# Both halves of the S5 channel groups through one scan of double width

## Chip, cores and metric

The kernel runs on one core of one Trainium2 chip. The metric is the device time of one execution in microseconds (us), of which the median of several runs is taken. All times inside an execution are counted from the start of its profiled span.

## What is computed

The reference is one inference step of a hybrid decoder trunk of two layers, for a prompt of 512 positions and 8 sample sequences of one position (520 columns). Layer 0 begins with the mixer that this change is about:

```python
# even l: parallel head groups from ONE combined input projection D -> [u 512 | q 512 | f 512 | i 512 | g 512]
#   A = S5 diagonal SSM (32 groups x 16 channels, each group drives a 64-dim complex state, associative scan, Re(C h) + D u, GLU)
#   B = HGRN2 (4 heads), concat(A, B) (1024) -> ONE output projection
bu_r = einsum('gpc,nlgc->nlgp', bbr, uf)      # and bu_i
h_t  = a * h_(t-1) + bu_t                     # complex, per group and state
y    = einsum('gcp,nlgp->nlgc', c_re, xr) - einsum('gcp,nlgp->nlgc', c_im, xi) + d * u
z    = gelu(y);  out = z * sigmoid(z @ w_glu + b_glu)
```

After it come cross-attention into 256 memory tokens and a ConvFFN, then layer 1 with a Conformer module, cross-attention and ConvFFN. The kernel also returns the last states.

## The kernel before

The columns stay on the free axis and channels on the 128 partitions, so x is a tile of 8 x 520 columns. Every projection multiplies in three parts: a weight block that comes by DMA (`wraw`) is rounded by ScalarE (`whi`) and the rest is kept (`wlo`, on VectorE, or on POOL for the blocks named in `GW`); per block that gives 48 matmuls of 256 or 264 columns on TensorE (L203).

S5 runs in `mixer0` (L409). The recurrence is cut into 64 blocks of 8 positions. `in_u` (L443) writes the projected channels u; `s5_u` (L635) sends them through DRAM into a tile U that has channel and position in block on the partitions. `s5_powers` (L494) makes the powers of the decay. The 32 channel groups are worked in two halves of 16, each by these steps:

- `s5_ops` (L560): X, six products of 128x1024 on VectorE; their transposes pM on TensorE (L578), copied to M by ScalarE; pK (L586), the block's kernel taps from X and cbd, copied to KT; eight shifted copies of KT by DMA (kts, L596), scaled into the Toeplitz operand TP by eight ScalarE copies (L599); and E (`s5_E`, L607), six instructions on POOL.
- `s5_scan` (L648): pS, M times U (L661); ScalarE copies them to W and Ws; then on VectorE the scan inside a block (seven W steps of five instructions), the scan over blocks (seven Bs steps of five instructions), the products m of powers and block states, half of them on POOL, and Hs. Four DMAs (L722) turn Hs into Hst. VectorE also makes the sample state (o_s_s).
- `s5_emit` (L725): pY, for each of 16 groups E times Hst (L737) plus TP times U (L738); ScalarE copies Y, which goes through DRAM (yd) into `s5_out` (L747).

`fill` (L811) puts ph blocks of the HGRN2 projection between these steps, 4 before the first half, 6 after its scan and 5 after the second, the rest after the last pY: the constant `FILL`. After all that `s5_glu` (L764) multiplies by w_glu (pg) and the HGRN2 part begins.

The order in which each engine takes its instructions is not the order of the lines. The framework sorts them when the kernel is built, by a time line of its own; each engine then takes its queue in order, and waits where an operand is late. SP issues the DMAs, and a DMA there waits for the one that was issued eight places before.

Of the kernel before, what the change touches and what calls it, by code (L numbers as in the profile page):

```python
# [9 lines left out]
F32 = mybir.dt.float32  # L10
F32R = mybir.dt.float32r
# [7 lines left out]
P = 128  # L19
# [3 lines left out]
NB = 8  # L23
# [14 lines left out]
ELATE = 0  # L38
# [8 lines left out]
FILL = (4, 6, 5)  # L47
# [54 lines left out]
def trunk(ctx, tc, I, O, dbg=None):  # L102
# [306 lines left out]
    def mixer0(nxt):  # L409
# [28 lines left out]
        with ExitStack() as es:  # L438
# [55 lines left out]
            def s5_powers():  # L494
# [48 lines left out]
                b1 = s5.tile([P, 16, 16], F32, tag="sop", name="b1", bufs=6)  # L543
                b2 = s5.tile([P, 16, 16], F32, tag="sop", name="b2", bufs=6)
# [14 lines left out]

            def s5_ops(hf):  # L560
                js = slice(hf * 8, hf * 8 + 8)
                X = [s5.tile([P, 8, 16, 8], F32, tag="sop", name=f"X{i}", bufs=6) for i in range(2)]
# [4 lines left out]
                t = s5.tile([P, 8, 16, 8], F32, tag="sop", name="tX", bufs=6)  # L567
# [6 lines left out]
                M = [s5.tile([P, 8, P], F32, tag="sop", name=f"M{i}", bufs=6) for i in range(2)]  # L574
# [5 lines left out]
                cbd = s5.tile([P, 2, 8, 32], F32, tag="cbd", name="cbd", bufs=1)  # L580
# [9 lines left out]
                TP = s5.tile([P, 16, 16, 8], F32, tag="TP", name="TP", bufs=1)  # L590
                for tq in range(2):
                    raw = s5.tile([P, 4, 256], F32, tag="sop", name="kts", bufs=6)
                    G.memset(raw[96:P], 0.0)
                    for t4 in range(4):
                        sh = 7 - (tq * 4 + t4)
                        nc.sync.dma_start(raw[0:P - sh, t4], KT[sh:P])  # L596
                    for t4 in range(4):
                        t8 = tq * 4 + t4
                        act(TP[:, :, :, t8], raw[:, t4].rearrange("p (g c) -> p g c", c=16), AF.Copy,  # L599
                            scale=tmask[:, t8:t8 + 1])  # L600
                ops[hf] = M, TP
                if not ELATE:
                    s5_E(hf)

            Es = {}

            def s5_E(hf):  # L607
                js = slice(hf * 8, hf * 8 + 8)
                full = [P, 8, 16, 8]
                E = []  # L610
                for g2 in range(2):
                    po = [POs[:, i, g2, js, :][:, :, None, :].to_broadcast(full) for i in range(2)]
                    cc = [sp[:, o:o + 512].rearrange("p (g j c) -> p g j c", g=2, c=16)[:, g2, js, :, None]
                          .to_broadcast(full) for o in (S_CA, S_CB)]
                    e = s5.tile([P, 8, 16, 8], F32, tag="sop", name=f"E{g2}", bufs=6)
                    t = s5.tile([P, 8, 16, 8], F32, tag="sop", name="tE", bufs=6)
# [4 lines left out]
                Es[hf] = E  # L621
# [13 lines left out]
            def s5_u(hf):  # L635
                U = s5.tile([P, 16, U5], F32, tag="U", name="U", bufs=2)
                G.memset(U[:, :, 0:NB], 0.0)
                G.memset(U[:, :, NB + NK5:U5], 0.0)
                Us[hf] = U
# [4 lines left out]
                nc.sync.dma_start(U[:, :, NB:NB + NK5], by_pos(ud, hf))  # L644
                nc.sync.dma_start(U[7:P:8, :, 0:NB], by_chan(uds, hf))
                nc.sync.dma_start(U[0:P:8, :, NB + NK5:U5], by_chan(uds, hf))

            def s5_scan(hf):  # L648
                M, TP = ops[hf]
                U = Us[hf]  # L650
                j0 = hf * 8
                js = slice(j0, j0 + 8)
                W = s5.tile([P, 2, 8, 64], F32, tag="WH", name="W", bufs=1)
                Ws = s5.tile([P, 2, 8, NB], F32, tag="Ws", name="Ws", bufs=1)
                for i in range(2):
# [3 lines left out]
                    for j in range(8):  # L659
                        for g2 in range(2):  # L660
                            T.matmul(pv[g2 * 64:g2 * 64 + 64, j // 4, j % 4, :],  # L661
                                     M[i][:, j, g2 * 64:g2 * 64 + 64], U[:, 2 * j + g2, 0:H5],
                                     start=True, stop=True)
                    for b in range(2):
                        act(Ws[:, i, b * 4:b * 4 + 4, :], pv[:, b, :, 0:NB], AF.Copy)
# [5 lines left out]
                a8r = PA[:, 0, 1, js]  # L671
                a8i = PA[:, 1, 1, js]
                nai = s5.tile([P, 8], F32, tag="nai", name="nai", bufs=2)
                ts(V, nai, a8i, -1.0, None, MUL)
                t1 = s5.tile([P, 2, 8, 8], F32, tag="t1", name="t1", bufs=2)
                t2 = s5.tile([P, 2, 8, 8], F32, tag="t2", name="t2", bufs=2)
# [7 lines left out]
                B = s5.tile([P, 2, 9, 8], F32, tag="Bs", name="Bs", bufs=1)  # L684
                G.memset(B[:, :, 0, :], 0.0)
                V.tensor_copy(B[:, :, 1, :], Wv[:, :, 7, :, 0])
                b8r, b8i = PA[:, 0, 8, js], PA[:, 1, 8, js]
                nbi = s5.tile([P, 8], F32, tag="nbi", name="nbi", bufs=2)
                ts(V, nbi, b8i, -1.0, None, MUL)
                for b in range(1, 8):  # L690
                    hp = B[:, :, b, :]
                    tt(V, t1[:, :, :, 0], hp, b8r[:, None, :].to_broadcast([P, 2, 8]), MUL)
# [4 lines left out]
                nc.sync.dma_start(O["p_s5"][:, :, js], B[:, :, 8, :])  # L697
                Hs = s5.tile([P, 2, 8, H5], F32, tag="HY", name="Hs", bufs=1)
                Hv = Hs[:, :, :, :NK5].rearrange("p i j (b q) -> p i q j b", q=8)
                f7 = [P, 7, 8, 8]  # L700
                Bv = [B[:, i, 0:8, :].rearrange("p b j -> p j b")[:, None].to_broadcast(f7) for i in range(2)]
                Pv = [PA[:, i, 1:8, js][:, :, :, None].to_broadcast(f7) for i in range(2)]
                m = [s5.tile([P, 2, 7, 8, 8], F32, tag="sop", name=f"m{i}", bufs=6) for i in range(2)]
                for k in range(2):
                    tt(G, m[1][:, k], Pv[k], Bv[1 - k], MUL)
                    tt(V, m[0][:, k], Pv[k], Bv[k], MUL)
                for i in range(2):
                    G.tensor_copy(Hv[:, i, 0], B[:, i, 0:8, :].rearrange("p b j -> p j b"))
                    tt(V, m[i][:, 0], m[i][:, 0], m[i][:, 1], ADD if i else SUB)
                    tt(V, Hv[:, i, 1:8], m[i][:, 0], Wv[:, i, 0:7], ADD)  # L710
                h0 = sp[:, S_H0:S_H0 + 256].rearrange("p (i j b) -> p i j b", i=2, b=NB)[:, :, js, :]
                V.tensor_copy(Hs[:, :, :, NK5:], h0)
                a1 = [PW[:, i, 1, js][:, :, None].to_broadcast(f3) for i in range(2)]
                sh = s5.tile([P, 2, 8, NB], F32, tag="shs", name="shs", bufs=1)
                cmul(V, sh[:, 0], sh[:, 1], h0[:, 0], h0[:, 1], a1[0], a1[1], t1[:, 0], t1[:, 1])
                tt(V, sh, sh, Ws, ADD)
                nc.sync.dma_start(O["s_s5"][:, :, js, :], sh)

                Hst = s5.tile([P, 2, 8, H5], F32, tag="WH", name="Hst", bufs=1)
                for i in range(2):  # L720
                    for g2 in range(2):
                        nc.sync.dma_start(Hst[i * 64:i * 64 + 64, g2], Hs[g2 * 64:g2 * 64 + 64, i])  # L722
                return Hst

            def s5_emit(hf, Hst):  # L725
                (M, TP), E = ops[hf], Es[hf]
                U = Us[hf]
                Y = s5.tile([P, 16, H5], F32, tag="HY", name="Y", bufs=1)
                for gq in range(2):
# [3 lines left out]
                    for g8 in range(8):  # L733
# [4 lines left out]
                        T.matmul(o, TP[:, g].rearrange("p c t -> p (c t)"), U[:, g, NB:U5],  # L738
# [8 lines left out]
            def s5_out(c):  # L747
                y = s5.tile([P, NT], F32, tag="sop", name="y5", bufs=6)
# [9 lines left out]
            def s5_split(z):  # L758
                t = s5.tile([P, 2, NT], F32R, tag="sop", name="zsp", bufs=6)
# [73 lines left out]
            fill(FILL[2])  # L833
            if ELATE:
                s5_E(1)
            s5_emit(1, H)
# [8 lines left out]
        with ExitStack() as es:  # L845
# [172 lines left out]

            for h in range(HH):
                prepare(h)  # L1020
# [673 lines left out]
```

## Time and profile before

| what | value |
|---|---|
| three runs | 1762.98, 1769.52, 1767.95 us; median 1767.95 us |
| profiled execution | 1769.77 us, its span 1768.0 us, mean granted TensorE clock 0.96 |
| TensorE (PE) matmuls busy | 1646.6 us, 93% of the span |
| PE weight loads | 1554.4 us, 88% |
| VectorE (DVE) | 995.9 us, 56% |
| ScalarE (ACT) | 810.9 us, 46% |
| POOL | 695.9 us, 39% |
| S5 part of the mixer | from the start to the first pg matmul at 203.17 us |

TensorE is the busy engine of the whole, so a change elsewhere counts only where TensorE stands still for it, or runs at the lower clock. The S5 part is 11% of the span, and it is there that the change moves work.

### The profile page before, as it was taken

The page shows a single profiled execution, that of the slowest core. Times are in us where ns is not written, and L with a number is a line of the kernel's source. Part 1 is how long each engine was busy: PE and PEld are TensorE (multiplying, and loading weights), DVE is VectorE, ACT ScalarE, POOL GpSimd, SP SyncE. Part 2 cuts the span into 40 slices and gives each one's busy share as a digit, 9 for nine tenths or more (in the row PEclk, how much of TensorE's full clock was granted, in tenths as well). Part 3 has the DMA queues.
Part 4 walks back from the last instruction along what each step waited for, and adds up shares of the span by engine and source line. Part 5 has one row for each costly group of instructions (what it writes and reads, how often), then busy time and mean ns, then how long its engine had stood idle before and what let it go on. Part 6 is the DMA issues. An engine that isn't in the chain of part 4 may idle for free. (4 is left out here: it accounts for less than half of the span.)

```text
span 1768.0 us, 32710 instructions
## 1 busy us (share of the span) xinstructions
PE 1646.6 (93%) x13008; PEld 1554.4 (88%) x13008; DVE 995.9 (56%) x1862; ACT 810.9 (46%) x1605; POOL 695.9 (39%) x699
## 2 busy tenths in 40 slices
PE   8978889999998999999999997798998999999996
PEld 8978866889788999999998995597788999999996
DVE  8677386885346633423348899748345731433345
ACT  6424434664245534333346666665245533323343
POOL 2544032312014716343434899223004725434343
PEclk9979798999999999999999999899999999999998
DMA  7332321275561233232331325143562223232321
GB/s 243 96 92 61 91 98 50 96 235 171 186 222 61 90 90 120 75 106 69 123 110 38 107 66 166 60 132 109 182 217 73 76 81 107 78 102 74 118 81 55
DMA packets 81392, 194.74 MB, mean 110 GB/s; under 512 B 21648, under 2 KB 31320, under 8 KB 81240
## 3 DMA queue, kind: packets, MB, share of 16 engines
q1 hardware_dynamic: 81240, 192.66, 34.4%
q8 instruction: 102, 1.67, 0.4%
q14 instruction: 50, 0.41, 0.1%
HBM read 176.67 MB, written 12.47 MB: 107 GB/s over the span
## 5 line engine op out<-in xcount | busy, mean ns | idle before, releaser
L130 ACT ACTIVATE whi<-wraw 128x512 fp32r<-128x512 f32 (+2 forms) x504 | 290.9, 587 | 520.0 <-PE pfo L203 128.0
L137 POOL TENSOR_TENSOR wlo<-wraw,whi 128x512 fp32r<-128x512 f32 x208 | 278.2, 1343 | 324.3 <-ACT whi L130 323.1
L137 DVE TENSOR_TENSOR wlo<-wraw,whi 128x512 fp32r<-128x512 f32 (+2 forms) x296 | 184.4, 634 | 171.8 <-ACT whi L130 163.5
L203 PE MATMUL pfb<-xnh,wlo 128*128 128x256 f32 (+1 forms) x672 | 135.9, 283 | 0.0
L203 PE MATMUL pfb<-xnl,whi 128*128 128x256 f32 (+1 forms) x672 | 135.2, 282 | 0.0
L203 PE MATMUL pfb<-xnh,whi 128*128 128x256 f32 (+1 forms) x672 | 135.2, 283 | 0.0
L203 PE MATMUL pfa<-xnh,wlo 128*128 128x256 f32 (+1 forms) x640 | 129.5, 283 | 0.0
L203 PE MATMUL pfa<-xnl,whi 128*128 128x256 f32 (+1 forms) x640 | 128.8, 282 | 0.0
L203 PE MATMUL pfa<-xnh,whi 128*128 128x256 f32 (+1 forms) x640 | 128.7, 282 | 0.0
L203 PE MATMUL pfo<-hlo,whi 128*128 128x256 f32 x604 | 122.1, 282 | 0.0
L203 PE MATMUL pfo<-hhi,wlo 128*128 128x256 f32 x604 | 121.5, 283 | 0.0
L203 PE MATMUL pfo<-hhi,whi 128*128 128x256 f32 x604 | 120.9, 282 | 0.0
L140 DVE SCALAR_TENSOR_TENSOR pcv<-cu,par,pcv 128x491 f32<-128x491 f32 (+19 forms) x160 | 109.5, 734 | 4.8 <-ACT pcv L130 3.4
L203 PEld LDWEIGHTS pfb<-xnh,whi 128*128 128x128 f32 x672 | 104.2, 188 | 0.0
L203 PEld LDWEIGHTS pfb<-xnh,wlo 128*128 128x128 f32 x672 | 104.2, 189 | 0.0
L203 PEld LDWEIGHTS pfb<-xnl,whi 128*128 128x128 f32 x672 | 104.1, 188 | 0.0
L203 PE MATMUL pf<-xnl,whi 128*128 128x256 f32 (+1 forms) x288 | 85.4, 306 | 20.0 <-DVE xnl L140 19.8
L203 PEld LDWEIGHTS pfa<-xnh,whi 128*128 128x128 f32 x640 | 99.3, 188 | 0.0
L203 PEld LDWEIGHTS pfa<-xnh,wlo 128*128 128x128 f32 x640 | 99.2, 189 | 0.0
L203 PEld LDWEIGHTS pfa<-xnl,whi 128*128 128x128 f32 x640 | 99.2, 188 | 0.0
L137 DVE TENSOR_TENSOR fa<-pfa,rstd 128x520 f32<-128x520 f32 x40 | 28.0, 699 | 125.2 <-PE pfa L203 125.2
L137 POOL TENSOR_TENSOR cc<-cc,ct 128x493 f32<-128x493 f32 (+15 forms) x74 | 94.1, 1275 | 4.9 <-ACT ct L130 1.1
(449 smaller groups left out, 4590.4 us busy)
## 6 DMA issues: line engine op xcount, KB each, us to landing
wraw<-w_ffn_in SPq DMA_DIRECT2D x88, 512.0 KB
ck<-cK SPq DMA_DIRECT2D x32, 512.0 KB
cv<-cV SPq DMA_DIRECT2D x32, 512.0 KB
wraw<-w_ffn_out SPq DMA_DIRECT2D x32, 384.0 KB
wraw<-w_ab_in SPq DMA_DIRECT2D x20, 512.0 KB
wraw<-w_ffn_out SPq DMA_DIRECT2D x32, 320.0 KB
wraw<-w_xk SPq DMA_DIRECT2D x16, 512.0 KB
wraw<-w_xv SPq DMA_DIRECT2D x16, 512.0 KB
```

Source lines behind the costliest of these rows:

```text
L130: A.activation(out, in_, f, **kw)
L137: e.tensor_tensor(out, a, b, op=op)
L140: V.scalar_tensor_tensor(out, in0, s, in1, op0=op0, op1=op1)
L203: T.matmul(ps[:, o:o + m], a[k], b[hv], start=first and k == 0 and i == 0, stop=last and k == n - 1 and i == 2)
```

## The change

Both halves go through the input matmuls first; then one scan runs at double width over all 32 groups, and both pY passes follow. TP is no longer a tile of its own: it lies in the tile of x, which is read again from DRAM before the HGRN2 part. U lies in tiles of six groups (three per half) from the pool of slabs. The pool `sop` has 9 buffers instead of 6 and takes cbd, Hs, Hst and Y too. `ELATE` goes, and E is written after the scan. Copies and products change engines: of the W copies those of the imaginary part go to VectorE, all m products go to VectorE, and the first columns of Hs to ScalarE.

```diff
-FILL = (4, 6, 5)
+FILL = (4, 6)
+NSOP = 9
...
+            TPt = [xt.rearrange("p c n -> p (c n)")[:, h * 2048:(h + 1) * 2048].rearrange(
+                "p (g c t) -> p g c t", g=16, c=16) for h in range(2)]
...
+                for g0 in range(0, 16, 6):
+                    n = min(6, 16 - g0)
+                    gs = slice(g0, g0 + n)
+                    U = slab("U", n=6 * U5).rearrange("p (g n) -> p g n", g=6)[:, :n]
+                    G.memset(U[:, :, 0:NB], 0.0)
+                    G.memset(U[:, :, NB + NK5:U5], 0.0)
+                    nc.sync.dma_start(U[:, :, NB:NB + NK5], by_pos(ud, hf)[:, gs])
+                    nc.sync.dma_start(U[7:P:8, :, 0:NB], by_chan(uds, hf)[:, gs])
+                    nc.sync.dma_start(U[0:P:8, :, NB + NK5:U5], by_chan(uds, hf)[:, gs])
...
-                        act(W[:, i].rearrange("p q (j b) -> p j b q", b=8)[:, b * 4:b * 4 + 4],
-                            pv[:, b, :, NB:].rearrange("p j (b q) -> p j b q", q=8), AF.Copy)
+                        if i:
+                            V.tensor_copy(dst, src)
+                        else:
+                            act(dst, src, AF.Copy)
...
-                f4 = [P, 2, 8, 8]
-                f3 = [P, 8, 8]
+                f4 = [P, 2, 16, 8]
+                f3 = [P, 16, 8]
...
-                    tt(G, m[1][:, k], Pv[k], Bv[1 - k], MUL)
-                    tt(V, m[0][:, k], Pv[k], Bv[k], MUL)
...
+                        tt(V, m[0][:, k], Pv[k], Bv[k], MUL)
+                        tt(V, m[1][:, k], Pv[k], Bv[1 - k], MUL)
...
-            s5_u(0)
-            fill(FILL[0])
-            s5_ops(0)
-            H = s5_scan(0)
+            fill(FILL[0])
+            s5_u(0)
+            s5_u(1)
+            for hf in range(2):
+                M, KT = s5_ops(hf)
+                s5_inputs(hf, M)
+                s5_toeplitz(hf, KT)
             fill(FILL[1])
-            if ELATE:
-                s5_E(0)
-            s5_u(1)
-            s5_emit(0, H)
-            s5_ops(1)
-            H = s5_scan(1)
-            fill(FILL[2])
-            if ELATE:
-                s5_E(1)
-            s5_emit(1, H)
+            Hsts, t1, t2 = s5_scan()
+            for hf in range(2):
+                s5_emit(hf, Hsts[hf], s5_E(hf))
+            s5_state(t1, t2)
             fill(len(todo))
...
+            nc.sync.dma_start(xt, I["xT"])
```

What this makes of the queues stands below for three engines.

SP, which issues the DMAs, around the ph blocks ahead of the first half. POs are powers that E needs, cbd is the operand of pK, kts the shifted copies of KT. Before:

```order
L644 DMA U<-ud 128x16x64
L645 DMA U<-uds 16x16x8
L646 DMA U<-uds 16x16x8
L180 DMA wraw<-w_ab_in 128x1024
L555 DMA POs<-PO 64x2x128 x4
L180 DMA wraw<-w_ab_in 128x1024 x3
L581 DMA cbd<-s5c 128x2x256
L596 DMA kts<-KT 121x256
```

(here cbd is that of the second half; the first one is issued at the kernel's start), and now:

```order
L555 DMA POs<-PO 64x2x128 x4
L180 DMA wraw<-w_ab_in 128x1024 x2
L648 DMA U<-ud 128x6x64
L649 DMA U<-uds 16x6x8
L650 DMA U<-uds 16x6x8
...
L650 DMA U<-uds 16x4x8
L587 DMA cbd<-s5c 128x2x256
L180 DMA wraw<-w_ab_in 128x1024
L604 DMA kts<-KT 121x256
```

The transfers of U moved from ahead of POs to behind two weights, are 18 in one row now, and the first half's cbd stands behind them.

ScalarE (ACT) at the copies for the first half of before, where TP<-kts are the Toeplitz copies and whi the weight roundings:

```order
L130 ACTIVATE KT<-pK 128x256
L130 ACTIVATE Ws<-pS 128x32
L130 ACTIVATE W<-pS 128x32x8
L130 ACTIVATE Ws<-pS 128x32
L130 ACTIVATE W<-pS 128x32x8
L130 ACTIVATE TP<-kts,cst 128x256 x4
L130 ACTIVATE Ws<-pS 128x32
L130 ACTIVATE W<-pS 128x32x8
L130 ACTIVATE Ws<-pS 128x32
L130 ACTIVATE TP<-kts,cst 128x256
L130 ACTIVATE W<-pS 128x32x8
L130 ACTIVATE TP<-kts,cst 128x256 x3
```

and of the change, where the same copies read x<-kts and M_1057 and the W copies from the fourth row on belong to the second half:

```order
L130 ACTIVATE M_1056<-pM 128x1024
L130 ACTIVATE x<-kts,cst 128x256 x2
L130 ACTIVATE M_1057<-pM 128x1024
L130 ACTIVATE x<-kts,cst 128x256 x3
L130 ACTIVATE W<-pS 128x32x8
...
L130 ACTIVATE x<-kts,cst 128x256
L130 ACTIVATE Ws<-pS 128x32
L130 ACTIVATE whi<-wraw 128x512
L130 ACTIVATE KT<-pK 128x256
L130 ACTIVATE x<-kts,cst 128x256
L130 ACTIVATE whi<-wraw 128x512
L130 ACTIVATE x<-kts,cst 128x256 x2
```

The copies from kts of one half now stand ahead of the other half's M and W, and those of the second half between the two roundings of a weight block.

POOL, from the kts memsets of the first half on (E and tE are `s5_E`, wlo the weight rests). Before:

```order
L593 MEMSET kts 32x1024 x2
L137 TENSOR_TENSOR E_970<-POs,sp 128x1024
L137 TENSOR_TENSOR tE<-POs,sp 128x1024
L137 TENSOR_TENSOR E_975<-POs,sp 128x1024
L146 TENSOR_SCALAR cbd<-cbd 128x256
L137 TENSOR_TENSOR E_970<-E_970,tE 128x1024
L137 TENSOR_TENSOR tE<-POs,sp 128x1024
L137 TENSOR_TENSOR E_975<-E_975,tE 128x1024
```

and now:

```order
L146 TENSOR_SCALAR cbd<-cbd 128x256
L146 TENSOR_SCALAR hf<-hf,lbt 128x520
L137 TENSOR_TENSOR wlo<-wraw,whi 128x512 x4
L137 TENSOR_TENSOR E_1653<-POs,sp 128x1024
L137 TENSOR_TENSOR tE<-POs,sp 128x1024
L137 TENSOR_TENSOR E_1658<-POs,sp 128x1024
L137 TENSOR_TENSOR tE<-POs,sp 128x1024
L137 TENSOR_TENSOR wlo<-wraw,whi 128x512 x2
L137 TENSOR_TENSOR E_1653<-E_1653,tE 128x1024
L146 TENSOR_SCALAR hf<-hf,lbt 128x520
L137 TENSOR_TENSOR E_1658<-E_1658,tE 128x1024
```

E of the first half moved from ahead of the scan to behind the weight rests of ph blocks 10 and 11, and its subtractions behind those of block 12.

## Rows read from the trace of the kernel before

**Rows 1.** Windows: us; PE, PEld, DVE, ACT, POOL busy (instructions); PEclk; DMA share; GB/s.

```profile
105.00:116.00 11.00, 1.85 (x17) 1.68 (x15) 11.00 (x17) 3.04 (x5) 4.14 (x3) 0.70 0.51 149
116.00:130.00 14.00, 14.00 (x66) 14.00 (x67) 4.52 (x6) 3.79 (x8) 4.73 (x5) 0.50 0.26 81
170.00:181.00 11.00, 0.06 (x1) 0.00 (x0) 10.81 (x25) 6.34 (x10) 1.44 (x3) 0.69 0.31 75
181.00:195.00 14.00, 13.78 (x65) 13.81 (x65) 0.00 (x0) 0.71 (x2) 0.00 (x0) 0.50 0.17 46
```

**Rows 2.** Waits of PE, 58 to 204 us: total us, times, longest us.

```profile
PE pY L737 <- DMA Hst<-Hs: 11.2, 1, 11.2
PE pY L737 <- POOL wlo L137: 9.1, 1, 9.1
```

**Rows 3.** Timeline of PE: start us, us, line, operation, xcount [idle before <-releaser].

```profile
36.16 0.41 PE L203 MATMUL ph<-xnh,whi 128*128 128x256 f32 x2
...
59.25 1.04 PE L578 MATMUL pM<-cst,X 128*128 128x128 f32 x8
...
61.17 3.43 PE L586 MATMUL pK<-cbd,X 128*128 128x32 f32 x30
64.53 3.73 PE L661 MATMUL pS<-U,M 128*64 128x72 f32 x64
...
203.17 1.38 PE L203 MATMUL pg<-zsp,whi 128*128 128x256 f32 x8 [0.85 <-ACT zsp L130]
```

**Rows 4.** Timeline of SP's DMA queue (the time is that of the issues).

```profile
34.16 2.13 SPq L645 DMA_DIRECT2D U<-uds  x1
...
56.11 4.99 SPq L180 DMA_DIRECT2D wraw<-w_ab_in  x3
64.64 0.60 SPq L581 DMA_DIRECT2D cbd<-s5c  x1
65.34 10.79 SPq L596 DMA_DIRECT2D kts<-KT  x8
...
112.20 2.45 SPq L722 DMA_DIRECT2D Hst<-Hs  x4
```

**Rows 5.** Timeline of ACT.

```profile
68.38 0.83 ACT L130 ACTIVATE TP<-kts,cst 128x256 f32<-128x256 f32 x1 [0.80 <-POOL tE L137]
71.44 0.82 ACT L130 ACTIVATE TP<-kts,cst 128x256 f32<-128x256 f32 x1 [2.23 <-DMA kts<-KT]
...
81.79 1.32 ACT L130 ACTIVATE TP<-kts,cst 128x256 f32<-128x256 f32 x2 [4.05 <-DMA kts<-KT]
82.89 1.17 ACT L130 ACTIVATE whi<-wraw 128x512 fp32r<-128x512 f32 x2
```

**Rows 6.** Timeline of DVE.

```profile
53.88 1.21 DVE L137 TENSOR_TENSOR X<-X,tX 128x1024 f32<-128x1024 f32 x1
...
78.26 0.29 DVE L137 TENSOR_TENSOR t<-W,PA 128x128 f32<-128x128 f32 x1
...
79.39 0.29 DVE L137 TENSOR_TENSOR t<-W,PA 128x128 f32<-128x128 f32 x1
...
168.09 2.06 DVE L137 TENSOR_TENSOR m<-PA,Bs 128x448 f32<-128x448 f32 x1
...
170.28 1.08 DVE L137 TENSOR_TENSOR m<-PA,Bs 128x448 f32<-128x448 f32 x1
```

**Rows 7.** Timeline of POOL.

```profile
64.53 1.95 POOL L137 TENSOR_TENSOR E<-POs,sp 128x1024 f32<-128x1024 f32 x1 [4.09 <-PE pK L586]
...
70.26 0.41 POOL L146 TENSOR_SCALAR cbd<-cbd 128x256 f32<-128x256 f32 x1
...
75.02 2.40 POOL L137 TENSOR_TENSOR E<-E,tE 128x1024 f32<-128x1024 f32 x1
...
116.63 2.68 POOL L137 TENSOR_TENSOR wlo<-wraw,whi 128x512 fp32r<-128x512 f32 x2 [0.75 <-ACT whi L130]
...
166.80 2.50 POOL L137 TENSOR_TENSOR m<-PA,Bs 128x448 f32<-128x448 f32 x2 [7.27 <-DVE Bs L137]
```

More of the change, by code (lines that the diff above doesn't have):

```diff
@@ L558, in mixer0, with sop @@
             ops = {}
+            def sop(shape, name):
+                return s5.tile(shape, F32, tag="sop", name=name, bufs=NSOP)
+            TPt = [xt.rearrange("p c n -> p (c n)")[:, h * 2048:(h + 1) * 2048].rearrange(
+                "p (g c t) -> p g c t", g=16, c=16) for h in range(2)]
             def s5_ops(hf):
                 js = slice(hf * 8, hf * 8 + 8)
-                X = [s5.tile([P, 8, 16, 8], F32, tag="sop", name=f"X{i}", bufs=6) for i in range(2)]
+                X = [sop([P, 8, 16, 8], f"X{i}") for i in range(2)]
                 full = [P, 8, 16, 8]
@@ L573, in s5_ops @@
                 tt(V, X[1], X[1], t, ADD)
-                M = [s5.tile([P, 8, P], F32, tag="sop", name=f"M{i}", bufs=6) for i in range(2)]
+                M = [sop([P, 8, P], f"M{i}") for i in range(2)]
                 for i in range(2):
@@ L579, in s5_ops @@
                     act(M[i].rearrange("p j n -> p (j n)"), ps, AF.Copy)
-                cbd = s5.tile([P, 2, 8, 32], F32, tag="cbd", name="cbd", bufs=1)
+                cbd = sop([P, 2, 8, 32], "cbd")
                 nc.sync.dma_start(cbd, I["s5c"][:, :, js])
@@ L589, in s5_ops, with s5_toeplitz @@
                 act(KT, pk[:, :256], AF.Copy)
-                TP = s5.tile([P, 16, 16, 8], F32, tag="TP", name="TP", bufs=1)
+                return M, KT
+            def s5_toeplitz(hf, KT):
                 for tq in range(2):
-                    raw = s5.tile([P, 4, 256], F32, tag="sop", name="kts", bufs=6)
+                    raw = sop([P, 4, 256], "kts")
                     G.memset(raw[96:P], 0.0)
@@ L643, in s5_u, with s5_inputs @@
                     nc.sync.dma_start(uds[f0:f0 + P, :], us[hf * 2 + q][:, LP:])
[L644 to L654, printed above, removed]
+                for g0 in range(0, 16, 6):
[7 more added lines that the diff above has]
+                    nc.sync.dma_start(U[0:P:8, :, NB + NK5:U5], by_chan(uds, hf)[:, gs])
+                    for g in range(n):
+                        Us[hf, g0 + g] = U[:, g]
+            W = s5.tile([P, 2, 8, 128], F32, name="W")
+            Ws = s5.tile([P, 2, 16, NB], F32, name="Ws")
+            def s5_inputs(hf, M):
                 for i in range(2):
@@ L696, in s5_scan @@
                     tt(V, B[:, :, b + 1, :], t1[:, :, :, 0], t2[:, :, :, 0], ADD)
[L697 to L699 removed]
+                nc.sync.dma_start(O["p_s5"], B[:, :, 8, :])
                 f7 = [P, 7, 8, 8]
[L701 removed]
@@ L711, in s5_scan @@
[L711 to L714, printed above, removed]
+                Hsts = []
+                for hf in range(2):
+                    js = slice(hf * 8, hf * 8 + 8)
+                    Hs = sop([P, 2, 8, H5], "Hs")
+                    Hv = Hs[:, :, :, :NK5].rearrange("p i j (b q) -> p i q j b", q=8)
+                    Bv = [B[:, i, 0:8, js].rearrange("p b j -> p j b")[:, None].to_broadcast(f7) for i in range(2)]
+                    Pv = [PA[:, i, 1:8, js][:, :, :, None].to_broadcast(f7) for i in range(2)]
+                    m = [sop([P, 2, 7, 8, 8], f"m{i}") for i in range(2)]
+                    for k in range(2):
+                        tt(V, m[0][:, k], Pv[k], Bv[k], MUL)
+                        tt(V, m[1][:, k], Pv[k], Bv[1 - k], MUL)
+                    h0 = sp[:, S_H0:S_H0 + 256].rearrange("p (i j b) -> p i j b", i=2, b=NB)[:, :, js, :]
+                    act(Hs[:, :, :, NK5:], h0, AF.Copy)
+                    for i in range(2):
+                        act(Hv[:, i, 0], B[:, i, 0:8, js].rearrange("p b j -> p j b"), AF.Copy)
+                        tt(V, m[i][:, 0], m[i][:, 0], m[i][:, 1], ADD if i else SUB)
+                        tt(V, Hv[:, i, 1:8], m[i][:, 0], Wv[:, i, 0:7, js], ADD)
+                    Hst = sop([P, 2, 8, H5], "Hst")
+                    for i in range(2):
+                        for g2 in range(2):
+                            nc.sync.dma_start(Hst[i * 64:i * 64 + 64, g2], Hs[g2 * 64:g2 * 64 + 64, i])
+                    Hsts.append(Hst)
@@ L715, in s5_scan, with s5_state @@
+                return Hsts, t1, t2
+            def s5_state(t1, t2):
+                h0 = sp[:, S_H0:S_H0 + 256].rearrange("p (i j b) -> p i j b", i=2, b=NB)
+                a1 = [PW[:, i, 1, :][:, :, None].to_broadcast([P, 16, 8]) for i in range(2)]
+                sh = s5.tile([P, 2, 16, NB], F32, name="shs")
                 cmul(V, sh[:, 0], sh[:, 1], h0[:, 0], h0[:, 1], a1[0], a1[1], t1[:, 0], t1[:, 1])
                 tt(V, sh, sh, Ws, ADD)
-                nc.sync.dma_start(O["s_s5"][:, :, js, :], sh)
@@ L719, in s5_scan @@
[L719 to L728, printed above, removed]
+                nc.sync.dma_start(O["s_s5"], sh)
@@ L729, in s5_emit @@
+            def s5_emit(hf, Hst, E):
+                Y = sop([P, 16, H5], "Y")
                 for gq in range(2):
@@ L747, in s5_out @@
             def s5_out(c):
-                y = s5.tile([P, NT], F32, tag="sop", name="y5", bufs=6)
+                y = sop([P, NT], "y5")
                 u = us[c]
```

60 lines of the change are left out of this document (24 added, 36 removed).

## Prediction

> **What bounds the kernel now.** I first read the stretch of the S5 mixer by windows, then TensorE's waits there, then the queues of the engines that it waits for. The mixer's own end is the first GLU matmul, pg, at 203.2 us [rows 3]; behind it the order of every engine is nearly the same in both programs, so I price the change by what it does to that moment. Up to 59.25 us nothing on TensorE changes: four ph blocks run without a gap from 36.16 to 59.25, 5.77 us each [rows 3]. Between 59.25 and 203.2 the reader is to see two holes: TensorE was busy 1.85 of 11 us before the first pY stage and 0.06 of 11 before the second, and both pY stages then ran at a granted clock of 0.50, which is the 1.2 GHz level [rows 1]. The waits name the two holes: 9.1 us put down to a weight split on POOL (the Hst transfers, issued from 112.20, belong to it too) and 11.2 us to Hst [rows 2, 4]. Each hole is the end of a scan of one half: inputs, scan on VectorE, Hst by DMA. A scan that sits behind other work is the resource that the change spends.
>
> **What it removes.** One of two scans goes: 35 instructions of W steps and 35 of block steps. At most that gives back the later hole, 11.2 us, and with pY0 and pY1 back to back the slow start of one of them: pY took 13.8 us at 0.50 [rows 1], and half of that, 6.9, if the clock were at its full level. With both holes gone the gain would be 9.1 + 11.2 = 20.3 us and something of the clock, say 22.
>
> **What it adds, in order of time.**
>
> *U and cbd on SP.* Before, six U transfers were issued early (the slowest issue 2.13 us, from 34.16) and lay beside the ph blocks [rows 4]; the first cbd was there from the start. Now 18 U transfers and then cbd stand behind the weight transfers of 56.11. No row has a U transfer of six groups. Each half moves what one half moved before: bounds are 2.1 us of issue per half (the one row) and 6.4 (three slabs at that price); 18 issues then last 4 to 13 us, and some wait for the weights and for each other. I take 10.5, so cbd is issued at 67.7. Its landing took between 3.0 us (kts, issued 65.34, used by ScalarE at 68.38) and 5.6 (cbd issued 64.64, used by POOL at 70.26) [rows 4, 5, 7]; 3.8 taken, nearer to the kts row since POOL was busy with E at the other. With 0.41 for POOL's multiply, pK of half 0 starts at 72, not 61. Cover for U and cbd is gone: TensorE has only pM and pS of half 0 (2 x 1.04 and 3.73 [rows 3]) in those 13 us.
>
> *Half 1 behind the kts transfers.* pK ends at 75.5, and its kts transfers start at 76.0. In the rows of before their copies on ScalarE began 3.0, 6.1 and (the last two) 16.45 us after the first issue [rows 4, 5]: so 79.0, 82.1 and 92.4. In ScalarE's new order M_1057 of half 1 stands behind the second copy, so with 0.82 for that copy and about 1 for M_1057 (1024 elements) pS of half 1 has its second operand at 84; half of pS, 1.9, is left, and it ends at T = 86. Bounds for T: 80 (U and cbd at their low ends) and 92. Before, the ph blocks resumed at 68.2 with half 0 alone done; so of the 27 us from 59.25 on some 12 are idle on TensorE, and new; the other 15 are two times pM, pS and once pK.
>
> *TensorE from T.* Six ph blocks and pK of half 1: 6 x 5.77 + 3.43 = 38 us, to 124.
>
> *The scan.* It starts when ScalarE has done five kts copies and two W copies, about 88.7. A W step took 1.13 us (78.26 to 79.39) [rows 6] in five instructions of 64 to 128 elements; the same five with twice the elements add at most as much again. I take 1.7, since 1024 elements took 1.21 us [rows 6], 0.0012 each, so that 64 or 128 more cost 0.07 to 0.14. Seven steps: 12. The seven block steps are at most a W step of before each: 6 taken. Between them stand six weight splits, and these wait for whi on ScalarE, which now stands behind the last kts copies: 92.4 plus copies for the first, and behind the kts copies of half 1 for the next. These start at pK of half 1 (T + 7.6), KT at 95.7, the last landing at 112.1; whi of block 8 is done at 114.3. That wait exists before (ScalarE idle 4.05 us for kts, whi at 82.89 [rows 5], VectorE late behind it), once per half; now one scan meets both. So the block steps end near 121; without that wait, and with six splits of 0.6 us, it would be 110.
>
> *m and Hs.* All eight m products are now VectorE's: 1.08 us alone [rows 6], so four per half are 4.3, with two subtractions, two t, hg and two Hs I estimate 8.5. Hs of half 0 is done at 129.5, Hst (2.45 us of issue [rows 4] and 2 more) lands at 134.
>
> *E on POOL.* Before, E was POOL's first work after kts, from 64.53 to 77.4 [rows 7], hidden under the scan. Now POOL's order puts the splits of blocks 10 and 11 ahead of it. The last of these needs whi, which on ScalarE stands behind the Hs copies (which wait for the block steps, 121) and behind hg (which waits for VectorE after the m products, 128). So wlo of block 11, at 1.34 [rows 7], ends near 132.5. Then four products of 1.95 (140.3), the two splits of block 12, whose whi is behind hq of block 8, itself behind the m products of half 1 on VectorE; two subtractions of 2.40 and one hf. That gives 149 when VectorE is on time and 152 when it is held up; I take 151. This is what is late next: pY0 does not start at 124, nor at 134 with Hst, but at 151. The cover that E had is gone, and a third hole of 27 us takes the place of the two of 11.
>
> VectorE and POOL at the same time: m took 2.06 us at 168.09, while POOL multiplied, and 1.08 at 170.28, when it did not [rows 6, 7]. By the rows alone, each product of half 1 costs between 1.08 and 2.06 us, so hq of block 8 and the splits of block 12 are 0 to 4 us late. The Trainium skill (SBUF — State Buffer, "SBUF: two separate sides") says that VectorE, when it reads two SBUF inputs, and POOL share a port pair that one instruction holds alone until it ends; by that rule each of these four products would wait out an E product of 1.95 us, and the sum would end 4 us later, near 212. The row at 168.09 agrees with it: about 1 us more, what was left of POOL's instruction.
>
> *pY and the rest.* pY0 runs at 0.50 as both did, 13.8 us, to 165. E of half 1 follows on POOL by 4 x 1.95 + 2 x 2.40 = 12.6 us, 163.6, and is in time. Between come 20 ph rows, 2.4; pY1 costs 6.9 to 13.8, 8.1 taken, because the clock has had a stage of TensorE work before it. 268 ph rows at 5.77/48 are 32.2. Sum: 165 + 2.4 + 8.1 + 32.2 = 207.7, against 203.2: 4.5 us later.
>
> The reload of x (2.1 MB) waits for the last pY and stands ahead of half 1's yd on SP. It is four weights' worth of bytes; three weight transfers left the queue in 4.99 us [rows 4], so some 7 to 8 us. It is hidden: 32.2 us of ph lie between pY1 and pg. Without that cover it would cost those 8. Twelve small U memsets against four, the W copies shared with VectorE and one o_s_s for two: nothing, all beside pS or the ph blocks.
>
> The profiled execution took 1769.77 us, 1.8 over the median of the runs. 1769.8 + 4.5 = 1774.3 on its scale, 1772.5 on the median's; I say **1773**.
>
> **Rivals.**
> *POOL gets to E in time (faster).* If kts lands sooner, or whi of blocks 8 to 11 are not held, POOL would reach E at 116 and pY0 would wait for Hst alone, 134. That is 17 us earlier, less a clock that stays low longer: 203.2 + 4.5 - 17 = 190.7, about 12.5 under before: 1755. For it: E was early in before and needs only POs and free tiles. Against it: POOL's new order is plain, and no row has the kts transfers faster. Chance 0.18.
> *Both holes go.* U, cbd and E all hidden: 22 us less, 1746. Every step above would have to be over-priced. Chance 0.07.
> *VectorE and POOL lock each other (slower).* The E products and m of half 1 run at the same time, from 132 on. If each waits for the other, hq of block 8, then whi and wlo of block 12, then the E subtractions move by 4 to 6 us more; the idle then is over 30 us, and if pY1 and the first ph rows also run at 0.50 that is 5.6 + 3 more: about 10 over the forecast, 15 over before, 1783. It decides from pY0 at 155 on. For it: 2.06 against 1.08, and two pY stages at 0.50. Against it: only what starts beside a POOL instruction pays, and the m products of half 0 come before E. Chance 0.30.
> The scan itself is single without doubt; the change does that.
>
> **How the numbers follow.** Forecast 0.45, the lock 0.30, E in time 0.18, both holes gone 0.07. A measurement of this kernel tells about 0.5%, 8.8 us, from no change. The two faster cases lie beyond that, 0.25 in all, of which 0.03 may fall short of it: 0.22. The lock gives 0.26 beyond and 0.04 inside; the forecast, +4.5 with T free by 6 us either way, gives 0.10 above 8.8. So slower 0.36, same 0.42, faster 0.22. The range leaves out the case of 22 us and reaches from the E rival, 1753 with T's low end, to the lock case with T's high end, 1791; the forecast's own range is 1765 to 1782.
>
> **What would show it.** Right: TensorE idle some 10 us between 59 and 86, pS of half 1 ending near 86; whi of blocks 7 and 8 on ScalarE behind kts copies; one idle piece of over 20 us before pY put down to POOL's E; no idle before pY1 over 2 us. Wrong: pY0 that starts with Hst, by 135; pK of half 0 before 66, which would mean that U and cbd cost little; pg before 195 or after 215.

## The result, and the profile after

| | before | after |
|---|---|---|
| median of 6 runs each | 1765.84 us (1762.98 to 1769.52) | 1776.66 us (1774.69 to 1777.26) |
| ratio to before | | 1.006, 95% interval 1.0044 to 1.0076 |
| span of the profiled execution | 1768.0 us | 1774.8 us |
| first pg matmul | 203.17 us | 218.68 us |

The change makes the kernel slower by 0.6%: it lies inside the predicted range, 3.7 us above the predicted 1773. The prediction counted a difference from 0.5% on; the interval, 0.44% to 0.76%, reaches to both sides of that. One of the six runs of a kernel below, E in the middle on VectorE, took 2034.08 us at a granted clock of 0.741 where its others had 0.953 to 0.961, and is left out of that kernel's median.

The two holes of before [rows 2] are gone, and four lines of waits stand in their place. TensorE's waits of after, 58 to 220 us (total us, times, longest us):

```profile
PE pY L751 <- POOL E L137: 23.8, 2, 22.7
PE pK L592 <- DMA cbd<-s5c: 9.9, 2, 8.7
PE pS L664 <- ACT M L130: 3.5, 1, 3.5
PE pS L664 <- DMA U<-uds: 1.8, 1, 1.8
```

The four sum to 39.0 us, against 20.3 of the two of before: 18.7 more, and pg is 15.5 us later. The windows of after (columns as in [rows 1]) show the clock's part:

```profile
59.00:73.00 14.00, 3.99 (x81) 3.63 (x79) 11.33 (x24) 4.32 (x10) 0.00 (x0) 0.80 0.57 144
73.00:92.00 19.00, 15.03 (x116) 14.34 (x117) 0.95 (x2) 5.22 (x7) 2.24 (x3) 0.59 0.20 59
136.00:159.00 23.00, 0.33 (x4) 0.10 (x1) 21.41 (x17) 7.02 (x12) 19.50 (x10) 0.57 0.39 106
159.00:173.00 14.00, 12.84 (x59) 12.64 (x60) 0.00 (x0) 0.71 (x2) 14.00 (x9) 0.50 0.09 33
```

After each hole TensorE runs near its lower level: pK at 73.48 took 7.17 us where before it took 3.43 [rows 3]. In PE's timeline of after (rows as in [rows 3]) the reader sees both holes at the end of a line:

```profile
73.48 7.17 PE L592 MATMUL pK<-cbd,X 128*128 128x32 f32 x32 [8.66 <-DMA cbd<-s5c]
...
88.95 2.19 PE L664 MATMUL pS<-U,M 128*64 128x72 f32 x32 [3.49 <-ACT M L130]
...
159.07 0.70 PE L751 MATMUL pY<-Hst,E 128*128 128x72 f32 x2 [22.74 <-POOL E L137]
...
218.68 0.64 PE L203 MATMUL pg<-zsp,whi 128*128 128x256 f32 x4
```

SP's queue of after answers to [rows 4]: the 18 U transfers from 56.85 on, cbd behind them, kts when pK is done:

```profile
56.85 0.43 SPq L648 DMA_DIRECT2D U<-ud  x1
...
70.06 0.61 SPq L587 DMA_DIRECT2D cbd<-s5c  x1
...
81.14 10.61 SPq L604 DMA_DIRECT2D kts<-KT  x8
```

VectorE of after answers to [rows 6]: the last copy ahead of the scan, which waits for ScalarE's Ws, the first row of a W step and of the next (1.66 us apart, 1.13 before), the weight split inside the scan that waits for ScalarE's whi, and the four products m of half 1:

```profile
97.96 0.62 DVE L672 COPY W<-pS 128x256 f32<-128x256 f32 x1 [3.48 <-ACT Ws L130]
...
102.32 0.42 DVE L137 TENSOR_TENSOR t<-W,PA 128x256 f32<-128x256 f32 x1
...
103.98 0.42 DVE L137 TENSOR_TENSOR t<-W,PA 128x256 f32<-128x256 f32 x1
...
116.83 0.69 DVE L137 TENSOR_TENSOR wlo<-wraw,whi 128x512 fp32r<-128x512 f32 x1 [5.96 <-ACT whi L130]
...
139.07 9.72 DVE L137 TENSOR_TENSOR m<-PA,Bs 128x448 f32<-128x448 f32 x4
```

POOL of after answers to [rows 7]: E, which began at 64.53 before, begins at 140.23, at 2.62 us a product instead of 1.95, and its first subtraction stands behind two splits that wait for ScalarE:

```profile
140.23 2.62 POOL L137 TENSOR_TENSOR E<-POs,sp 128x1024 f32<-128x1024 f32 x1
...
147.99 2.62 POOL L137 TENSOR_TENSOR tE<-POs,sp 128x1024 f32<-128x1024 f32 x1
153.37 3.16 POOL L137 TENSOR_TENSOR wlo<-wraw,whi 128x512 fp32r<-128x512 f32 x2 [2.76 <-ACT whi L130]
156.48 2.53 POOL L137 TENSOR_TENSOR E<-E,tE 128x1024 f32<-128x1024 f32 x1
```

pg is 15.5 us later, but the span of the profiled execution only 6.8. The first part of what comes back is pg itself. In before it began 8 us after pY1, a stage at 0.50, and stalled for operands that are made from Y. TensorE's waits of before, 203 to 219 us:

```profile
PE pg L203 <- DVE u L137: 2.1, 1, 2.1
PE pg L203 <- ACT zsp L130: 0.9, 1, 0.9
```

This window of before (columns as in [rows 1]) runs from its first matmul to the next stage, pp:

```profile
203.10:218.80 15.70, 13.51 (x96) 13.23 (x97) 10.32 (x21) 12.48 (x25) 0.00 (x0) 0.89 0.31 94
```

and the same stage of after runs without a gap at the full level:

```profile
218.50:230.20 11.70, 11.70 (x99) 11.70 (x99) 8.54 (x19) 8.83 (x20) 0.00 (x0) 1.00 0.42 132
```

4 us return there, and the stage took 11.5 to 11.9 us in all the variants below, so this part is firm. Another 4.6 are gone by the end of the span (the first pq matmul is 9.1 us later than before, the first po 6.7), but these are not clear of the scatter: from the first pp matmul to the end of the span before took 1549.2 us, after 1544.6, and the variants below 1538 to 1548. The profiled run of before took 1769.77 us, 3.9 above its median, that of after 1776.61, its median. By the medians the two kernels are 10.8 us apart, not 6.8.

### The profile page after: what moved, and what is told of

Same layout as the page of the kernel before. It is cut to its first block, busy times and chain, and to the rows that moved or that the text cites. A ratio compares the mean times of both kernels' runs of the same rounds, so it can differ in the third digit from the quotient of the medians.

```text
span 1774.8 us, 32656 instructions
## 1 busy us (share of the span) xinstructions
PE 1638.2 (92%) x13008; PEld 1548.1 (87%) x13008; DVE 985.7 (56%) x1788; ACT 810.1 (46%) x1607; POOL 692.7 (39%) x698
## 5 line engine op out<-in xcount | busy, mean ns | idle before, releaser
L203 PE MATMUL pfo<-hhi,wlo 128*128 128x256 f32 x604 | 121.4, 282 | 0.0
L203 PE MATMUL pf<-xnl,whi 128*128 128x256 f32 (+1 forms) x288 | 85.1, 305 | 22.6 <-DVE xnl L140 22.6
```

The lines of the kernel that those rows point to most:

```text
L203: T.matmul(ps[:, o:o + m], a[k], b[hv], start=first and k == 0 and i == 0, stop=last and k == n - 1 and i == 2)
```

## Experiments

All ratios are to the kernel before, run on the same chip in the same job; three rounds each. A time set beside the change's 1776.66 us, or a time of the first four beside the others, compares different jobs; the kernel before had medians of 1765.01 to 1766.14 us in them, 1765.84 beside the change. The first four undo one suspected cost each.

**E ahead of the scan.**

```diff
                 s5_toeplitz(hf, KT)
+                Es.append(s5_E(hf))
...
-                s5_emit(hf, Hsts[hf], s5_E(hf))
+                s5_emit(hf, Hsts[hf], Es[hf])
```

> E of each half is made right behind that half's kts transfers, ahead of the scan; all else as in the changed kernel. Theory (E stands last in front of pY): pY of the first half starts with Hst, near 142 us instead of 159, the m products of the second half lose their 2.4 us each, and the run takes 1761 us, 13 to 17 under the change. Rival (the front, cbd behind the 18 U transfers and the second half behind kts, sets the time and E only fills it): 1775 to 1778. Rival (POOL is only moved: the kts memsets of the second half wait behind E): pS of the second half ends later than 91 us, and less than 5 us are gained.

1774.35 us, ratio 1.0044 (1.0032 to 1.0056). The wait of pY for E is gone, yet only some 2 us came back. TensorE's waits, 58 to 220 us:

```profile
PE pS L664 <- ACT M L130: 9.4, 1, 9.4
PE pY L751 <- DMA Hst<-Hs: 9.0, 1, 9.0
PE pK L592 <- DMA cbd<-s5c: 8.4, 1, 8.4
```

pS of half 1 ended at 108.6 instead of 91.1: E held tiles of the nine in `sop`, X of half 1 waited 6.03 us for POOL's E, and on ScalarE six kts copies lay between the two M copies of half 1 (84.40 and 97.53). But with no E beside them the four m products of half 1 took 3.4 us, not 9.72:

```profile
151.13 3.38 DVE L137 TENSOR_TENSOR m<-PA,Bs 128x448 f32<-128x448 f32 x4
```

**Weight splits off POOL.**

```diff
-GW = (10, 11, 12, 13, 14)
+GW = ()
```

> GW is empty, so VectorE makes all weight rests and POOL has only E in front of pY; E stays behind the scan. If the rests of blocks 10 to 12 ahead of E are what makes it late, pY starts 8 us earlier or more (POOL's 3.2 us for two rests between E's products and subtractions, 2.8 us of waiting for them, and the 2 us before) and the run takes about 1768. If E waits for its buffers (those of m, free after Hs at 138 us) its first product starts where it did, near 140, pY 3 to 6 us earlier: 1771 to 1774. If VectorE's ten more rests of 0.6 us delay the scan, nothing is gained.

1776.17 us, ratio 1.0049 (1.0032 to 1.0067): nothing gained, pY waits 22.6 us for E. POOL's timeline says why: its queue is free at 125.9, and E still cannot go on, first for tiles that VectorE's m and Hs hold, then because its subtractions stand behind hf, which comes from VectorE by way of ScalarE:

```profile
125.87 2.39 POOL L137 TENSOR_TENSOR E<-POs,sp 128x1024 f32<-128x1024 f32 x1
140.49 2.35 POOL L137 TENSOR_TENSOR tE<-POs,sp 128x1024 f32<-128x1024 f32 x1 [12.23 <-DVE Hs L137]
...
157.18 0.77 POOL L146 TENSOR_SCALAR hf<-hf,lbt 128x520 f32<-128x520 f32 x1 [9.21 <-ACT hf L130]
157.92 4.64 POOL L137 TENSOR_TENSOR E<-E,tE 128x1024 f32<-128x1024 f32 x2
```

The edit also put ten more splits on VectorE: Hs of half 0 was done at 141.2, where in the change it was done at 138.0. There POOL's queue let E begin at 140.23, so at its start the splits kept E for some 2 us at most, and the tiles for the rest.

**cbd in a tile of its own**, so that it need not wait for a buffer of `sop`.

```diff
-                cbd = sop([P, 2, 8, 32], "cbd")
+                cbd = s5.tile([P, 2, 8, 32], F32, tag="cbd", name="cbd", bufs=1)
```

> cbd has a tile of its own again, so the first half's cbd comes at the kernel's start and pK of the first half does not wait for it. Theory (front plus E): pK starts near 64 instead of 73.5 us, the kts transfers some 12 us earlier (pK at the full clock too), and as everything down to E hangs on them, the run is 8 to 12 us shorter: about 1766. Rival (E behind the splits of blocks 10 to 12, which wait for the ph blocks on TensorE): those blocks end earlier as well, so the gain is no smaller; only if POOL's queue were bound by weights would it be under 3 us: 1774 to 1777.

1767.82 us, ratio 1.0004 (0.9993 to 1.0015): 8.8 us below the change's median. pK starts at 59.5, pS of half 1 ends at 79 (91.1 in the change). The other hole grew:

```profile
PE pY L751 <- POOL E L137: 28.6, 2, 28.3
```

**U's transfers ahead of the first ph blocks.**

```diff
-            fill(FILL[0])
             s5_u(0)
             s5_u(1)
+            fill(FILL[0])
```

> Both s5_u stand ahead of the four ph blocks as before, cbd still behind them on SP. Theory (U and cbd transfers in the way): cbd is then issued near 61 us instead of 70, pK of the first half starts near 65, and the run gains what cbd in a tile of its own gains, 8 to 12 us: about 1766. If the six U transfers per half only take the place of weight transfers there, weights come late and the four ph blocks wait: 1775 or more.

1769.57 us, ratio 1.0017 (1.0003 to 1.0032); pK starts at 63.9, pY waits 28.9 us for E. So the front costs 7 to 10 us (8.8 and 7.1 by the medians, 9.9 and 7.6 by the ratios), and the wait for E is left in both. Whether it is a second cost is what the next four ask: they join the edits.

**E ahead of the scan and cbd apart** (the edits of the first and the third).

> Edit: s5_E of each half right behind its Toeplitz operands, and cbd in a tile of its own (both earlier edits together). Theory A (two separate costs: the late cbd at the front, and E not ready at pY; E ahead of the scan alone gained nothing because the two E tiles of half 0 and seven tiles of half 1 and its cbd are ten tiles for nine buffers; with cbd elsewhere they are nine): pS of half 1 ends at 79 to 83 as with cbd alone (79.0), the scan ends near 121, pY of half 0 starts at 133 to 140 with no wait over 3 us for POOL's E, what is left of its wait is for Hst; pg starts at 191 to 197; time 1755 to 1762 us. Theory B (POOL's E products delay half 1's operands whatever the buffers, by the lock with VectorE's X or by the POOL queue ahead of the memsets): pS of half 1 ends after 95, pY0 after 148, time 1766 to 1772 us. Theory C (the gain comes but is taken back later): pg before 198, time 1764 to 1768 us.

1762.55 us, ratio 0.9987 (0.9975 to 0.9999): 14.1 us below the change, where the two edits alone gave 2.3 and 8.8. By the ratios, each to the kernel before in its own job, it is 12.9 against 2.8 and 9.9: the two costs add, and that they make up more together is not shown. The trace does show one taking up part of the other: with cbd alone TensorE was done with its other work at 124.4 instead of 136.3, but pY0 started only 6.4 us earlier (152.65 against 159.07), as the wait for E grew by the rest. The time is half a microsecond above A's range, and not all of A held: pS of half 1 ended at 97.0, as B said, pY started at 142.0, between the two, and pg at 206.2 instead of 191 to 197. The new wait is 13.0 us of pM for VectorE's X of half 1, and VectorE's timeline shows the cause in the power products before X:

```profile
62.59 2.03 DVE L137 TENSOR_TENSOR cm<-PA 128x32 f32<-128x32 f32 x2
...
66.53 4.56 DVE L137 TENSOR_TENSOR cm<-PA 128x32 f32<-128x32 f32 x2
...
71.35 0.36 DVE L137 TENSOR_TENSOR cm<-PA 128x64 f32<-128x64 f32 x2
...
72.74 1.22 DVE L137 TENSOR_TENSOR X<-PR,BB 128x1024 f32<-128x1024 f32 x1
```

Two products of 128x32 took 4.56 us, two of twice the size 0.36 us a little later. Between lies the end of POOL's E:

```profile
64.44 2.00 POOL L137 TENSOR_TENSOR tE<-POs,sp 128x1024 f32<-128x1024 f32 x1
66.41 4.63 POOL L137 TENSOR_TENSOR E<-E,tE 128x1024 f32<-128x1024 f32 x2
```

In the kernel with cbd alone, no E beside it, X began 12 us earlier, but there the build also put it ahead of these products:

```profile
60.27 1.22 DVE L137 TENSOR_TENSOR X<-PR,BB 128x1024 f32<-128x1024 f32 x1
...
64.91 0.29 DVE L137 TENSOR_TENSOR cm<-PA 128x32 f32<-128x32 f32 x2
```

So the better measure is the change itself, where the same products stand in a row with no E beside them:

```profile
60.27 0.29 DVE L137 TENSOR_TENSOR cm<-PA 128x32 f32<-128x32 f32 x2
...
62.69 0.17 DVE L144 TENSOR_SCALAR nbi<-PA 128x16 f32<-128x16 f32 x1
```

From the first of them to the last they took 2.6 us there and 10.2 here (62.59 to 72.83); these 7.6 us are E's.

**cbd apart and U first.**

> Edit: cbd in a tile of its own and the transfers of U ahead of the first HGRN2 block. Theory A: both edits remove the same wait (8.8 and 7.1 us alone), so they do not add: pS of half 1 ends at 73 to 79, pY0 still waits over 20 us for POOL's E and starts at 147 to 153, time 1764 to 1768 us. Rival (two different costs): they add, 1759 to 1762 us, pY0 before 146.

1767.11 us, ratio 1.0013 (1.0002 to 1.0023): they do not add; pY0 at 150.8 after 28.7 us for E. (pS of half 1 ended at 87, not 73 to 79, since it waited 9.1 us for an M copy on ScalarE.)

**All three.**

> Edit: all three (E ahead of the scan, cbd in its own tile, U's transfers first). Theory A: no wait of pY0 for POOL over 3 us; the scan starts at 82 to 88; pY0 starts when the HGRN2 blocks or Hst end, at 128 to 137; pg at 186 to 194; time 1752 to 1760 us, 0 to 4 us below the kernel without U first. Theory B (E delays half 1): pY0 after 145, time 1764 to 1770 us.

1764.04 us, ratio 0.9994 (0.9983 to 1.0005): no E wait, but pY0 at 142.0 and 11.6 us of waiting for X again, so it lies above A's forecast and at the edge of B's.

**Only half 0's E early, cbd apart.**

> Edit: cbd in a tile of its own, only half 0's E ahead of the scan, half 1's E where it was. Theory A: pY0 starts at 133 to 140 without a wait for POOL; E of half 1 (4 products at 1.95 to 2.6 us, 2 subtractions) runs beside m of half 1, so m takes 1.5 to 2.5 us each (0.85 each with no E beside it), and pY of half 1 waits 3 to 12 us for POOL's E; time 3 to 8 us above the kernel with both E's early. Rival (m is slow for another reason than E on POOL): m of half 1 at 2.4 us each in the kernel with both E's early too.

1765.02 us, ratio 1.0 (0.9988 to 1.0012), 2.5 us above both E's early, not 3 to 8; pY0 started at 143.96, not by 140, after 9.5 us for Hst, and pY1 waits 4.6 us for E. A's forecast for m missed too: E of half 1 fell behind hf in POOL's queue and started only at 153.3, after m, which so kept its 0.84 us each. The rival for m fell in the kernel with both E's early, where the four took 3.39 us, not 9.6.

The last four look for a better place for E.

**E in the middle, on POOL** (with cbd apart).

```diff
                 M, KT = s5_ops(hf)
+                if hf:
+                    Es.append(s5_E(0))
                 s5_inputs(hf, M)
                 s5_toeplitz(hf, KT)
+            Es.append(s5_E(1))
```

> Edit: cbd in a tile of its own; half 0's E put between half 1's operand products X and its input matmuls, half 1's E behind its Toeplitz operands, both still on POOL. Theory L (in the kernel with E early and cbd apart, half 1's X came 12 us late, at 72.7 instead of 60.3, because POOL's E products beside VectorE's small operations made each of those wait for the end of a POOL product): X of half 1 is done by 70, pS of half 1 ends at 79 to 86, no wait of pY0 for POOL over 3 us, pY0 starts at 133 to 140, time 1756 to 1761 us. Rival (X of half 1 was late for its buffers): X of half 1 starts after 70 here too, pY0 at 140 to 145, time 1761 to 1764 us.

1758.4 us, ratio 0.996 (0.9946 to 0.9974; 5 runs): 0.4% below the kernel before and 1% below the change, the best kernel of this study, though under the 0.5% bound. All of L's numbers hold: X of half 1 done at 68, pS at 80.5, pY0 at 136.3 with this wait and none for POOL:

```profile
PE pY L751 <- DMA Hst<-Hs: 8.0, 1, 8.0
```

pg starts at 199.6, ahead of before. E now meets the scan; a W step beside it takes 9.85 us instead of 1.66 (the first rows of two steps, and one of POOL's instructions in between):

```profile
104.78 0.81 DVE L137 TENSOR_TENSOR t<-W,PA 128x256 f32<-128x256 f32 x1
...
114.63 0.43 DVE L137 TENSOR_TENSOR t<-W,PA 128x256 f32<-128x256 f32 x1
```

```profile
107.36 2.44 POOL L137 TENSOR_TENSOR E<-E,tE 128x1024 f32<-128x1024 f32 x1
```

**E in the middle, on VectorE.**

```diff
-                    tt(G, e, po[0], cc[0], MUL)
-                    tt(G, t, po[1], cc[1], MUL)
-                    tt(G, e, e, t, SUB)
+                    tt(V, e, po[0], cc[0], MUL)
+                    tt(V, t, po[1], cc[1], MUL)
+                    tt(V, e, e, t, SUB)
```

> Edit: as the kernel with E in the middle, with E's products and subtractions on VectorE instead of POOL. Theory L: an operation of 128x1024 takes 1.2 us on VectorE as X's do, 12 of them 14.6 us, most of it in the 11 us in which VectorE waits for pS of half 1; nothing locks, so pY0 starts at 131 to 139 and the time is 0 to 4 us below the kernel with E in the middle on POOL. Rival (VectorE is the chain, and 14.6 us more on it are paid in full): the block steps end 10 to 15 us later than with cbd alone (121), pY0 after 143, time 1763 to 1768 us.

1769.65 us, ratio 1.0029 (1.001 to 1.0048): 11 us slower than on POOL. L's forecast missed; the rival held in its signs, and its time was still 1.7 us too low. The operations took 1.2 us as expected, but the block steps ended at 137.6 (121.4 with cbd alone, 124.2 with E on POOL), and pY0 waited 21.5 us for Hst. Some 7 us of E stood ahead of the first whole step, and VectorE's waits, 80 to 150 us, name the rest:

```profile
DVE wlo L137 <- ACT whi L130: 12.6, 3, 5.9
DVE t L137 <- ACT Ws L130: 6.2, 1, 6.2
DVE E L137 <- ACT x L130: 4.8, 1, 4.8
```

The splits between the scan's steps waited for whi, and ScalarE had put kts copies ahead of whi. With E on POOL the list for the same stretch (80 to 150 us) has no wlo at all:

```profile
DVE t L137 <- ACT Ws L130: 6.3, 1, 6.3
DVE W L672 <- ACT Ws L130: 4.4, 1, 4.4
```

How much of the 11 us is E on VectorE and how much the order that the build gave ScalarE stays open: the edit changed both.

**And cbd of both halves in one early transfer.**

```diff
-                cbd = sop([P, 2, 8, 32], "cbd")
...
+            cbd = s5.tile([P, 2, 16, 32], F32, name="cbd")
+            nc.sync.dma_start(cbd, I["s5c"])
+            ts(G, cbd[:, 1], cbd[:, 1], -1.0, 0.0, MUL, ADD)
             fill(FILL[0])
```

> Edit: as the kernel with E in the middle on VectorE, and cbd of both halves loaded in one transfer ahead of the first HGRN2 block (the tile shs takes KT's memory). If the cbd of half 1, issued on SP behind half 0's eight kts transfers (at 80), still holds up work: pK of half 1 runs by 75 and the second kts transfers are issued 8 to 12 us earlier, the whi copies on ScalarE with them, time 1 to 5 us below the kernel without it. Rival (hidden): within 1 us of it.

1766.33 us, ratio 1.0003 (0.9992 to 1.0013), 3.3 us less, as expected: pK of half 1 ran from 67.1 to 72.1, the second kts transfers were issued 7 us earlier (88.32 against 95.18), and VectorE waited 4.3 us for whi instead of 12.6. So cbd of the second half, behind eight kts transfers on SP, was probably not hidden either; as the intervals of the two ratios overlap, the time alone does not show it.

**And both input matmuls ahead of both Toeplitz operands.**

```diff
+            s5_inputs(0, M)
+            KT = s5_kt(0, X)
+            X, M = s5_ops(1)
+            s5_inputs(1, M)
+            s5_toeplitz(0, KT)
```

> Edit: as the kernel before in this list, and both halves' input matmuls ahead of both halves' Toeplitz operands (so that ScalarE's M copies do not stand behind its x copies, which wait for kts). If that order matters: pS of half 1 ends at 72 to 78 (79 to 86 without), the scan's first step starts at 80 to 85, pY0 at 127 to 135, time 1 to 5 us below the kernel before in this list. Rival (the scan is held by the HGRN2 splits that VectorE does between its steps, and these by ScalarE's x copies): the scan starts earlier and ends at the same time, time within 1.5 us.

1767.88 us, ratio 1.0009 (0.9993 to 1.0025): 1.6 us above the one before in this list, the interval of each holding the other's ratio. As the rival said, the scan started earlier and ended at about the same time: pS of half 1 ended at 72.1, 11 us earlier, and the first whole step began at 91.5 instead of 108.3, but VectorE then waited 14.2 us for whi inside the scan, and pY0 started at 145.0 instead of 146.4.

## Why the prediction was right, and where its sum was not

**The time** was 1773 and came out as 1776.66; by the median that is on the slower side, to which 0.36 had been given ("same" had 0.42). By the text's own bounds the sum behind it failed twice: pg came at 218.7, past the 215 that should prove it wrong, and pY0 at 159, past the 155 from which the rival of the lock was to decide. That the time still fits is in part luck. The sum set the time by pg alone, which was to be 4.5 us late and was 15.5; it had no term for the 4 us that came back in the pg stage, and it counted from 1767.95, the median of three runs, where six runs have 1765.84. From the kernel before, 10.8 us were lost and some 5 forecast. The ends of the range do not follow from the numbers given with them either: with T free by 6 us, 1755, 1783 and 1773 give 1749, 1789 and 1767 to 1779, not 1753, 1791 and 1765 to 1782.

**The 11 us by which pg missed** (218.7 against 207.7) are mostly pY0's start, 8.0 us late. pY0 and the 20 ph rows behind it took 21.1 us (159.07 to 180.20) where 16.2 were forecast: pY0 waited 1.1 us for E's second tile, 72 pY matmuls instead of 64 stood in it, and the ph rows, too, still ran near the lower level (4.4 us instead of 2.4). pY1, with the 56 matmuls left, gave 1.7 back.

**U and cbd on SP.** Right, with cbd issued at 70.06 (67.7 forecast) and pK at 73.48 (72). That it costs was shown twice by taking it away: 8.8 and 7.1 us.

**pK.** Mis-sized: 3.43 us, from a row at the full level, for a stage that came out of a hole: 7.17.

**Half 1 behind the kts transfers.** Right in kind; T was 91.1, not 86, of which pK's length is 3.7 and its start 1.5.

**The scan.** A W step of 1.66 us against 1.7, and the block steps of after ended at 129.9 (121 forecast); the start moved it, 98.6 instead of 88.7. Of these 9.9 us T is 5.1, and 3.5 are VectorE's wait for the last Ws, which on ScalarE stood behind the seventh kts copy (97.15), where the forecast had counted five. The splits between the steps did wait for whi behind kts copies: 5.96 and 2.00 us.

**E on POOL.** The largest term was right in place and kind, one hole of 22.7 us put down to E (27 forecast, as TensorE itself arrived later, at 136 instead of 124). The reason was half right. The prediction held POOL's queue of splits to be what keeps E; with the splits gone nothing was won, because tiles held by m and Hs, and hf in the same queue, kept it as well. With E moved out of all of them and cbd apart, 14 to 18 us came back; beside the kernel with cbd alone, 5.3 to 9.4 of them are E's.

**The lock** was a rival with 0.30. Its mechanism is seen, but it is not what made pY0 late. m of half 1 took 2.43 us each (9.72 for four), against 0.85 with no E beside them. The Trainium skill (SBUF — State Buffer, "SBUF: two separate sides") has VectorE with two SBUF inputs and POOL hold a shared port pair alone, one instruction at a time; these rows agree, and so do the 4.56 us of two 128x32 products beside E. The rival's price of 10 us over the forecast is about what pg shows, but by coincidence: E's first product began at 140.23 instead of 132.5, so 7.7 of pY0's 8.0 us were lost before E met m, down the chain from pK and the scan. Beside m, E's four products took 10.4 us where 7.8 were forecast; that 2.6 is what the rows put down to the lock, with some part of the 2.76 us for which POOL's split waited for whi. pY0 was not later by these as well, because it started on the first of E's two tiles (159.0; the second was done at 162.1). On the way there a split on POOL took 5.58 us beside the scan (130.78) and the one before it 1.37, but the next waited for whi all the same. No run takes the lock away by itself, so what it costs in time is not shown.

**The clock.** pY0 at 0.50 was right, as was pY1 at a higher level: its 56 matmuls took 6.4 us (180.20 to 186.6), where 8.1 were forecast for 64. The reload of x was hidden as forecast: from pY1's end to pg it took 32.1 us, the 268 ph rows at full speed 32.2.

**"E in time" (0.18)** was possible in this program after a small edit, not in the change as built.

## What to carry to other kernels

When two passes are merged, list what one pass hid of the other: here the first half's scan hid E, and the early cbd and U of the first half cost nothing because there was other work beside them. When one cost is taken away, look at which wait grew: here TensorE was free 12 us earlier with cbd alone, and half of that went into a longer wait for E, so the two repairs are worth judging together. And price a delay at the end of the program as well as at the end of its stage, since stages behind it may run closer together and at a higher clock: here 4 of 15.5 us came back in the next stage.

## What the runs showed of the hardware

A VectorE operation with two SBUF operands beside a POOL operation pays for POOL's length, not for its own: two 128x32 products took 4.56 us beside E and 0.29 us without, and a W step 9.85 us against 1.66. It goes both ways; POOL's products took 2.62 us beside m and 1.95 alone.

On VectorE the same 128x1024 product took 1.2 us instead of 1.95, and nothing of E could lock; yet the kernel was 11 us slower. A lock beside the chain may thus be cheaper than the work on the chain, though the edit changed ScalarE's order too, and its part is not told apart.
